# Residual with tokens on partitions, tokens stationary in the output and down projections, and another order in the prologue

## The chip, the cores and the metric

The kernel runs on one core of a Trainium2 chip. The core has a matrix engine (TensorE, PE in the profile), a vector engine (VectorE, DVE), an activation engine (ScalarE, ACT), a general engine (GpSimd, POOL) and a queue for transfers (SyncE, SP), which work side by side and wait for each other by semaphores. The metric is the time of one launch on the device in microseconds; several runs are made and their median is given.

## The reference

Two encoder layers over 256 tokens of 2048 features, float32. In each layer the normalised residual goes through one input projection (4608 columns), whose columns feed two groups of eight heads; the normalised outputs of the groups go through one output projection into the residual; a gated feed-forward part with a width-3 convolution over the tokens follows.

```python
for l in range(DEPTH):                                  # DEPTH = 2
    h = rms_norm(x, ln1_g[l])
    qa, ka, va, qb, kb, vb = jnp.split(h @ w_in[l], cuts, axis=-1)
    oa = neighborhood_attention(norm(qa), norm(ka), va, rpb[l])
    ob = windowed_gqa_sink(rope(norm(qb)), rope(norm(kb)), vb, sink[l])
    o = jnp.concatenate([rms_norm(oa, on_a[l]), rms_norm(ob, on_b[l])], axis=-1)
    x = x + o @ w_out[l]
    h2 = rms_norm(x, ln2_g[l])
    u = depthwise_conv(h2 @ w_up[l], conv_w[l], conv_b[l])
    gate, up = u[..., :D_FF], u[..., D_FF:]             # D_FF = 5632
    x = x + (jax.nn.silu(gate) * up) @ w_down[l]
```

(`norm` stands here for the RMS norm of each head with its gain.)

## The kernel before

**Products in two parts.** Every operand of the four projections is split into a high part and a low part, which both have the shorter mantissa of the format that PE takes in one pass (float32r): ACT copies the high part, DVE subtracts it to get the low part (`split`, lines 96 to 104). A product of two such operands is the sum of three products: high x high, high x low, low x high.

**Layout.** The residual `x` lies with features on partitions: 16 blocks of 128 features, each 256 tokens wide. `prep_x` (L123) makes the operands `xs[k]` of the next projection from block k, with the norm's gain folded in, and `square_x` (L118) adds the block's squares into `acc_x`; the norm's factor is applied after the projection. `stat_cols` (L130) and `stat_bcast` (L137) get that factor by products with a matrix of ones, as a column for each token or spread over the partitions.

**Two forms of product.** In the input projection (`q_win`, L363) the tokens are stationary: 128 tokens of `xs[k]` are loaded as weights, and 512 columns of the weight block move, three products for each block of features and token tile. The result has tokens on partitions. In the output, up and down projections (`q_wout` L413, `q_up` L452, `q_down` L495) the weights are stationary, 128 x 128 of them, and the tokens move. `two` (L356) issues there a pair: the high weights meet high and low tokens (512 columns), and the low weights meet the high tokens (256 columns). The sums come out in two halves of a bank, with features on partitions, and are added by `add_halves` (L444) or by two additions (`fin`, L512).

**The stream of weight blocks.** Weights come as blocks ("quanta") of at most 1 MiB in the order of `quanta`: in each layer nine jobs of four blocks for the input projection (`JOBS`, first the keys and values of group b), eight blocks of output projection for group b and eight for a, then four chunks of 11 feed-forward blocks (two weight blocks each), each followed by 16 smaller blocks of the down projection. One more up block is put before each chunk's down projection, so that PE has work while the last gate is computed; where there is none, in the last chunk, the halves of the first three down blocks are used in another order (`late`). `load` (L554) keeps three blocks in flight, `split_w` (L565) splits half a block four halves ahead of its use, and the loop at L620 walks through the halves ("steps"). Smaller work, such as the attention of one head, is put between the halves with `at` (L353). The order on each engine is planned when the kernel is built, from these priorities and a simulated timeline, so that a piece may stand a few instructions after the place where it was written.

**The gate.** `glu` (L474) takes an up block's pair of halves, adds them, multiplies by the norm's factor (on POOL, but for a layer's last block), convolves, gates and splits the result into `gs[f]`.

**Prologue.** `load_x` brings the residual in pieces between the first weight blocks, all on SP's queue. `prep_x` splits the 16 blocks on ACT and DVE, POOL squares them, and `rope_base` (L145) computes the rotary tables with some 40 DVE operations, placed at block 1. The first job, `kvb`, needs these tables when it is done.

**Tail.** In the last layer `fin` adds and stores two feature blocks at a time, and single ones at the very end.

Of the kernel before, what the change touches and what calls it, by code (L numbers as in the profile page):

```python
# [18 lines left out]
P = 128  # L19
L = 2  # L20
# [12 lines left out]
CH = 11  # L33
NCH = NF // CH
EPS = 1e-6
NEG = -1e30
JOBS = ("kvb", "qb0", "qb1", "va0", "ka0", "qa0", "qa1", "ka1", "va1")
# [9 lines left out]
def encoder_kernel(  # L47
# [18 lines left out]
    x = const.tile([P, KD, T], F32, name="x")  # L66

    def load_x(k, n):
        nc.sync.dma_start(out=x[:, k:k + n, :], in_=a["x"][:, k:k + n, :])  # L69
# [13 lines left out]
    def rsqrt(ps, inv_n, dst, tag):  # L83
        """dst = 1 / sqrt(ps * inv_n + EPS)"""
        n = list(dst.shape)
        v = work.tile(n, F32, name="v_" + tag, bufs=1)
        nc.vector.tensor_scalar(v, ps, inv_n, EPS, op0=ALU.mult, op1=ALU.add)
        nc.vector.tensor_scalar(dst.bitcast(I32), v.bitcast(I32), -0.5, 1597463007.0,
                                op0=ALU.mult, op1=ALU.add)
        t = work.tile(n, F32, name="t_" + tag, bufs=1)  # L90
        for _ in range(3):
            nc.vector.scalar_tensor_tensor(t, dst, -0.5, dst, op0=ALU.mult, op1=ALU.mult)
            nc.vector.tensor_mul(t, t, v)
            nc.vector.scalar_tensor_tensor(dst, t, 1.5, dst, op0=ALU.add, op1=ALU.mult)

    def split(hi, lo, src, scale=None):
        """hi + lo = src (* scale), each with float32r's mantissa"""
        if scale is None:
            nc.scalar.activation(hi, src, AF.Copy)  # L99
            nc.vector.tensor_sub(lo, src, hi.bitcast(F32))  # L100
        else:
            nc.scalar.activation(hi, src, AF.Copy, scale=scale)
# [3 lines left out]
    def add_square(acc, src, first, on_pool=False):  # L106
        sq = acc if first else work.tile([P, T], F32, name="sq", bufs=2)
        if on_pool:
            nc.gpsimd.tensor_mul(sq, src, src)
        else:  # L110
            nc.scalar.activation(sq, src, AF.Square)  # L111
# [6 lines left out]
    def square_x(k, on_pool=False):  # L118
        if k == 0:
            st["acc"] = act.tile([P, T], F32, name="acc_x")  # L120
        add_square(st["acc"], x[:, k, :], k == 0, on_pool)

    def prep_x(l, which, k, squares=True):  # L123
        """the operands of the next projection from one block of the residual"""
        xs[k] = act.tile([P, 2, T], F32R, name=f"xs{k}")
        split(xs[k][:, 0], xs[k][:, 1], x[:, k, :], ln_g[:, which, l, k:k + 1])
        if squares:
            square_x(k)

    def stat_cols(l):  # L130
        ps = psum.tile([P, TT], F32, name="pv", bufs=1)
        for tt in range(TT):
            mm(ps[:, tt:tt + 1], st["acc"][:, tt * P:(tt + 1) * P], ones[:, 0:1], True, True)
        st["r1"] = act.tile([P, TT], F32, name="r1")
        rsqrt(ps, 1.0 / D, st["r1"], "c2")

    def stat_bcast(acc, n, dst):  # L137
        ps = psum.tile([P, T], F32, name="pv", bufs=1)
        mm(ps, ones, acc, True, True)
        rsqrt(ps, 1.0 / n, dst, "b")  # L140

# [1 line left out]
    rope = {}  # L143

    def rope_base():  # L145
        """cos and sin of positions * inv, with the angle reduced exactly"""
# [3 lines left out]
        tmp = work.tile([P, 4, HD], F32, name="qtok", bufs=3)  # L150
# [6 lines left out]
        # 2 pi to 80 bits, in pieces of 7 bits  # L157
# [15 lines left out]

        nearest(k1, r, 4096.0)
        nc.vector.tensor_copy(r1, r)
        for c in pieces[:5]:
            less(r1, k1, c)
        nearest(k2, r1, 1.0)
        for c in pieces:
            less(r, k1, c)  # L180
            less(r, k2, c)
        nearest(k1, r, 1.0)
        for c in pieces[:5]:
# [13 lines left out]
    def rope_tables(l):  # L197
        """the rotation with the gains of the QK norm and the score scale folded in"""
# [18 lines left out]
    def evac_v(ps, cols, key):  # L217
        v = act.tile([P, TT, len(range(*cols.indices(512)))], F32, name="v_" + key[0], bufs=1)
        for tt in range(TT):
            nc.scalar.activation(v[:, tt, :], ps[tt][:, cols], AF.Copy, scale=st["r1"][:, tt:tt + 1])  # L220
        V[key] = v

    def evac_qk(ps, nh, kind):
        """QK norm and, for group b, the rotation; tokens on partitions"""
# [4 lines left out]
        for tt in range(TT):  # L229
            q = work.tile([P, 4, HD], F32, name="qtok", bufs=3)[:, :nh, :]  # L230
            nc.scalar.activation(q, ps[tt][:, :n].rearrange("p (h d) -> p h d", h=nh), AF.Copy,
# [117 lines left out]
    quanta = []  # L349
    late = []  # L350
# [10 lines left out]
    cur = {}  # L361

    def q_win(l, j, u):  # L363
        def body(q, half, hi, lo):
            if u == 0 and half == 0:
                cur["in"] = psum.tile([P, TT, 512], F32, name="mm", bufs=2)
            ps = [cur["in"][:, tt] for tt in range(TT)]
            hv, lv = (w.rearrange("p (k n) -> p k n", k=2) for w in (hi, lo))
            for tt in range(TT):
                for kk in range(2):  # L370
                    k = 4 * u + 2 * half + kk
                    x_h, x_l = (xs[k][:, i, tt * P:(tt + 1) * P] for i in range(2))
                    mm(ps[tt], x_l, hv[:, kk], k == 0, False)
                    mm(ps[tt], x_h, hv[:, kk], False, False)
                    mm(ps[tt], x_h, lv[:, kk], False, k == KD - 1)
# [4 lines left out]
            if u == 2 and j == 0:  # L380
                rope_tables(l)
            if u == 3 and j == 0:
                stat_cols(l)
            if u == 3:
                done_win(q, l, j, ps)
# [27 lines left out]
    def q_wout(l, grp, npair):  # L413
        def body(q, half, hi, lo):
            g = 0 if grp == "a" else 1
            if half == 0:
                cur["out"] = psum.tile([P, 2, 2, T], F32, name="mm", bufs=2)
            ps = cur["out"]
            hv, lv = (w.rearrange("p (k j n) -> p k j n", k=4, j=2) for w in (hi, lo))
            for j in range(2):  # L420
                for hh in range(4):
                    h = 4 * half + hh
                    two(ps[:, j], hv[:, hh, j], lv[:, hh, j], os[g * NH + h], h == 0, h == NH - 1)
            if half == 0:
                return
            if npair == 0:
                st["ro"] = act.tile([P, T], F32, name="ro", bufs=2)
                stat_bcast(acc_o[grp], NH * HD, st["ro"])
            if npair == KD // 2 - 1:
                with tc.high_priority(offset=4 * AHEAD_PRIO):  # L430
                    add_out(l, grp, 2 * npair, ps)
            else:
                add_out(l, grp, 2 * npair, ps)
        return body

    def add_out(l, grp, n, ps):
        t = add_halves(ps)
        nc.vector.tensor_mul(t, t, st["ro"][:, None, :].to_broadcast([P, 2, T]))
        nc.vector.tensor_add(x[:, n:n + 2, :], x[:, n:n + 2, :], t)
        if grp == "a":  # L440
            for j in range(2):
                prep_x(l, 1, n + j)

    def add_halves(ps):  # L444
        t = work.tile([P, 2, T], F32, name="prob", bufs=2)
        nc.scalar.activation(t, ps[:, :, 0], AF.Copy)  # L446
        nc.vector.tensor_add(t, t, ps[:, :, 1])  # L447
        return t
# [3 lines left out]
    def q_up(l, f, u):  # L452
        def body(q, half, hi, lo):
# [8 lines left out]
            if half == 0:  # L462
                return
            if u == 1 and f == 0:
                st["r2"] = act.tile([P, T], F32, name="r2")
                stat_bcast(st["acc"], D, st["r2"])
            if u == 1 and f == NF - 1:
                with tc.high_priority(offset=4 * AHEAD_PRIO):
                    glu(l, f, ps, nc.vector)
            elif u == 1:  # L470
                glu(l, f, ps, nc.gpsimd)
        return body

    def glu(l, f, ps, eng):  # L474
        t = add_halves(ps)
# [4 lines left out]
        eng.tensor_copy(ux[:, :, 1:r], ux[:, :, T:T + r - 1])  # L480
        eng.tensor_copy(ux[:, :, T + r:T + 2 * r - 1], ux[:, :, r + 1:2 * r])
# [13 lines left out]
    def q_down(l, c, n):  # L495
        def body(q, half, hi, lo):
            k0 = half * (CH // 2 + 1)
            hv, lv = (w.rearrange("p (k n) -> p k n", n=P) for w in (hi, lo))
            last = l == L - 1 and c == NCH - 1 and n >= KD - 2
            if (n % 2 == 0 or last) and half == 0:  # L500
                cur["dn", n // 2, last and n] = psum.tile([P, 2, 2, T], F32, name="mm", bufs=2)
            ps = cur["dn", n // 2, last and n]
            for kk in range(hv.shape[1]):
                k = k0 + kk
                two(ps[:, n % 2], hv[:, kk], lv[:, kk], gs[c * CH + k], k == 0, k == CH - 1)
            if half == 1 and last:
                fin(l, c, n, 1, ps[:, n % 2:n % 2 + 1])
            elif half == 1 and n % 2 == 1:
                fin(l, c, n - 1, 2, ps)
        return body  # L510

    def fin(l, c, n, m, ps):  # L512
        xv = x[:, n:n + m, :]
# [194 lines left out]
```

## Time and profile before

| what | value |
|---|---|
| median of 3 runs | 2141.22 us (2140.93 to 2141.46) |
| span of the profiled execution | 2139.1 us; the profile gives no time outside of the span for it |
| PE busy | 2119.9 us (99%) |
| DVE, ACT, POOL busy | 1566.4, 1179.8, 313.1 us |
| moved by DMA | 395.94 MB, mean 185 GB/s |

The span runs from the first to the last instruction; the runs' time is that of the launch, 2.1 us longer in the median. "Busy" is the time in which an engine executed at least one instruction. A group of instructions is given with its source line, its output and inputs by the program's names (`mm<-xs,whi`: the bank `mm` from the operands `xs` and `whi`), its shape, its count, its busy time and the mean duration of one. Products overlap on PE, so the mean duration of one is longer than the distance from one to the next; the distance is read from a stretch's length and its count. A product of plain float32 operands stands in the trace as two records.

### The profile page before, as it was taken

The numbers are of one execution on the slowest core, as the hardware profiler recorded it, in microseconds if no ns is written. First come the engines' busy times: TensorE is split into PE (matmuls) and PEld (weight loads), VectorE is DVE, ScalarE is ACT, GpSimd is POOL, SyncE is SP. The second block draws the span as 40 slices with busy tenths as digits, with TensorE's granted clock in tenths as the row PEclk, the third lists the DMA queues.
The fourth block names the chain that finished last, engine by engine and source line by source line (L and its number), as shares of the span: only waits on it lengthen the run. The fifth ranks groups of instructions, "written<-read, shape, count | busy, mean of one in ns | idle before, by whom it ended". The sixth has DMA issues, their size and how long they took to land.

```text
span 2139.1 us, 31086 instructions
## 1 busy us (share of the span) xinstructions
PE 2119.9 (99%) x11740; PEld 1848.2 (86%) x11740; DVE 1566.4 (73%) x2439; ACT 1179.8 (55%) x1744; POOL 313.1 (15%) x373
## 2 busy tenths in 40 slices
PE   7999999999999999999999999999999999999999
PEld 5888888888888888888888888888888888888888
DVE  8776789776677677667877667897766766776775
ACT  4665556654555455455656655565545545554553
POOL 5000013210121022012100100122102201110210
PEclk9999999999999999999999999999999999999999
DMA  7535555545654654654664454555465556546544
GB/s 260 191 131 179 175 179 179 197 166 197 208 185 166 220 181 168 212 191 157 199 215 176 141 187 164 177 182 194 168 212 191 179 176 217 192 161 219 188 157 167
DMA packets 64950, 395.94 MB, mean 185 GB/s; under 512 B 7840, under 2 KB 10144, under 8 KB 29088
## 3 DMA queue, kind: packets, MB, share of 16 engines
q1 hardware_dynamic: 64800, 393.96, 54.1%
q8 instruction: 92, 1.51, 0.3%
q14 instruction: 58, 0.48, 0.1%
HBM read 391.83 MB, written 2.10 MB: 184 GB/s over the span
## 4 chain that ended last, share of the span: by engine, by line
PE 98%; DVE 1%; DMA 1%; SPq 0%; ACT 0%; issue 0%
PE mm L81 95%; PE pv L81 1%; PE S L81 1%; PE tr L264 1%; DMA raw<-in_w_in 1%; PE tr L325 0%; PE tr L81 0%; DVE xs L103 0%; DVE wlo L100 0%; PE tr L320 0%; SPq L69 0%; SPq L561 0%; PE tr L317 0%; DVE qtok L172 0%; DVE qtok L153 0%
## 5 line engine op out<-in xcount | busy, mean ns | idle before, releaser
L100 DVE TENSOR_TENSOR wlo<-raw,whi 128x1024 fp32r<-128x1024 f32 (+3 forms) x817 | 944.8, 1157 | 496.6 <-ACT whi L99 490.0
L99 ACT ACTIVATE whi<-raw 128x1024 fp32r<-128x1024 f32 (+3 forms) x817 | 795.6, 975 | 803.3 <-PE mm L81 656.2
L81 PE MATMUL mm<-xs,whi 128*128 128x512 f32 x2816 | 976.5, 391 | 0.0
L81 PE MATMUL mm<-xs,wlo 128*128 128x256 f32 x2816 | 788.8, 280 | 0.0
L81 PE MATMUL mm<-mid,whi 128*128 128x512 f32 x1920 | 670.1, 392 | 0.0
L81 PEld LDWEIGHTS mm<-xs,whi 128*128 128x128 f32 x2816 | 526.5, 187 | 115.4
L81 PE MATMUL mm<-mid,wlo 128*128 128x256 f32 x1920 | 541.7, 282 | 0.0
L81 PEld LDWEIGHTS mm<-xs,wlo 128*128 128x128 f32 x2816 | 532.2, 189 | 0.1
L81 PEld LDWEIGHTS mm<-mid,whi 128*128 128x128 f32 x1920 | 360.7, 188 | 75.6 <-DVE prob L447 0.4
L81 PE MATMUL mm<-whi,xs 128*128 128x512 f32 x1152 | 369.7, 399 | 6.9 <-ACT whi L99 6.9
L81 PEld LDWEIGHTS mm<-mid,wlo 128*128 128x128 f32 x1920 | 362.9, 189 | 0.2
L478 POOL TENSOR_TENSOR halo<-prob,r 128x512 f32<-128x512 f32 x86 | 112.0, 1303 | 1094.4 <-DVE prob L447 1069.7
L81 PEld LDWEIGHTS mm<-whi,xs 128*128 128x128 f32 x1152 | 216.5, 190 | 50.5 <-ACT whi L99 7.2
L81 PE MATMUL mm<-wlo,xs 128*128 128x512 f32 x576 | 230.1, 399 | 8.1 <-DVE wlo L100 8.1
L488 DVE SCALAR_TENSOR_TENSOR pT<-halo,conv,pT 128x256 f32<-128x256 f32 x352 | 149.6, 486 | 6.4
L81 PEld LDWEIGHTS mm<-wlo,xs 128*128 128x128 f32 x576 | 109.2, 190 | 32.6 <-DVE wlo L100 10.4
L486 ACT ACTIVATE pT<-halo,conv 128x256 f32<-128x256 f32 x176 | 96.3, 595 | 40.7 <-POOL halo L478 40.4
L480 POOL COPY halo<-halo 128x6 f32<-128x6 f32 x86 | 85.0, 989 | 5.5
L447 DVE TENSOR_TENSOR prob<-prob,mm 128x512 f32<-128x512 f32 x120 | 81.6, 680 | 0.0
L113 POOL TENSOR_TENSOR acc_x<-acc_x,sq 128x256 f32<-128x256 f32 x60 | 55.8, 930 | 144.7 <-ACT sq L111 142.4
L446 ACT ACTIVATE prob<-mm 128x512 f32<-128x512 f32 x120 | 69.7, 581 | 0.0
L113 POOL TENSOR_TENSOR acc_b<-acc_b,sq 128x256 f32<-128x256 f32 x14 | 16.4, 1171 | 284.1 <-ACT sq L111 284.1
(132 smaller groups left out, 987.4 us busy)
## 6 DMA issues: line engine op xcount, KB each, us to landing
raw<-in_w_up SPq DMA_DIRECT2D x176, 1024.0 KB, 4.8
raw<-in_w_down SPq DMA_DIRECT2D x128, 704.0 KB, 4.1
raw<-in_w_in SPq DMA_DIRECT2D x71, 1024.0 KB, 4.8
raw<-in_w_out SPq DMA_DIRECT2D x32, 1024.0 KB, 4.8
bias<-in_bias SPq DMA_DIRECT2D x16, 160.0 KB, 2.3
out<-x SPq DMA_DIRECT2D x7, 256.0 KB, 4.1
x<-in_x SPq DMA_DIRECT2D x3, 512.0 KB, 9.7
raw<-in_w_in SPq DMA_DIRECT2D x4, 256.0 KB, 5.9
```

Source lines behind the costliest of these rows:

```text
L81: nc.tensor.matmul(ps, lhsT, rhs, start=start, stop=stop, skip_group_check=True)
L99: nc.scalar.activation(hi, src, AF.Copy)
L100: nc.vector.tensor_sub(lo, src, hi.bitcast(F32))
L113: nc.gpsimd.tensor_add(acc, acc, sq)
L264: nc.tensor.transpose(ps[:, j, tt * P:(tt + 1) * P], qn[tt][:, p + j, :], ident)
L446: nc.scalar.activation(t, ps[:, :, 0], AF.Copy)
L447: nc.vector.tensor_add(t, t, ps[:, :, 1])
L478: eng.tensor_mul(ux[:, :, r:r + T], t, st["r2"][:, None, :].to_broadcast([P, 2, T]))
L480: eng.tensor_copy(ux[:, :, 1:r], ux[:, :, T:T + r - 1])
L486: nc.scalar.activation(y[:, j, :], ux[:, j, r:r + T], AF.Identity, scale=w1, bias=b)
L488: nc.vector.scalar_tensor_tensor(y[:, j, :], ux[:, j, o:o + T], w, y[:, j, :], op0=ALU.mult, op1=ALU.add)
```

## The change

The residual lies with tokens on partitions (two tiles of 128 tokens, 2048 wide). The output and down projections take the input projection's form: `three` issues, for two blocks of the contraction at a time, the products high x high, low x high and high x low, each with 128 tokens stationary and 512 columns of weights moving, into two banks. The result is added to the residual straight from the banks, by `add_x`. `whole_x` follows where a quarter of the residual (512 features, `nb`) is complete: `square_x` sums its squares on ACT by row, and `turn_x` transposes it on PE, 128 x 128 at a time, into a bank from which `prep_x` makes the operands of the next projection. `stat_x` computes the norm's factor; for the up projection it spreads it over the partitions with one product.

The down projection has chunks of 12, 12, 12 and 8 feed-forward blocks and weight blocks of 1 MiB throughout; `late` is gone, and the last chunk takes its first two quarters in turns. The gate's multiplication is on DVE for all blocks.

In the prologue the transposed input comes as an input of its own (`xT`), half of it on ACT's queue; ten small products of ones stand ahead on PE; the first job is `va0`, which needs no tables; the residual itself is loaded later, held behind the issue of certain weight loads (`issue_after`), and is squared on ACT; `rope_base` yields pieces that are spread over blocks 4 and 5; the first job's eviction is put off to block 7.

```diff
-JOBS = ("kvb", "qb0", "qb1", "va0", "ka0", "qa0", "qa1", "ka1", "va1")
+JOBS = ("va0", "kvb", "qb0", "qb1", "ka0", "qa0", "qa1", "ka1", "va1")
...
+    x = const.tile([P, TT, D], F32, name="x")
...
+    def square_x(nb):
...
+        for tt in range(TT):
+            sq = work.tile([P, 512], F32, name="sqx", bufs=1)
+            nc.scalar.activation(sq, x[:, tt, nb * 512:(nb + 1) * 512], AF.Square,
+                                 accum_out=st["ss"][:, tt, nb:nb + 1])
+
+    def turn_x(l, which, nb):
+        for k in range(4 * nb, 4 * nb + 4, 2):
+            ps = psum.tile([P, 2, T], F32, name="S", bufs=2)
+            for j in range(2):
+                for tt in range(TT):
+                    nc.tensor.transpose(ps[:, j, tt * P:(tt + 1) * P], x[:, tt, (k + j) * P:(k + j + 1) * P], ident)
+            for j in range(2):
+                prep_x(l, which, k + j, ps[:, j, :])
+
+    def stat_x(which):
+        v = work.tile([P, TT], F32, name="ssum", bufs=2)
+        nc.vector.reduce_sum(v, st["ss"], axis=AX.X)
+        st["r1"] = act.tile([P, TT], F32, name="r1")
+        rsqrt(v, 1.0 / D, st["r1"], "c2")
+        if which == 1:
...
+            mm(ps, ones, d[:, 0:TT].rearrange("p t d -> p (t d)"), True, True)
...
+    def three(ps, terms, hv, lv, first, last):
+        n = len(terms)
+        for x_part, w in ((0, hv), (1, hv), (0, lv)):
+            for tt in range(TT):
+                for i, x2 in enumerate(terms):
+                    mm(ps[:, tt], x2[:, x_part, tt * P:(tt + 1) * P], w[:, i],
+                       first and w is hv and x_part == 0 and i == 0, last and w is lv and i == n - 1)
...
             if u == 3:
-                done_win(q, l, j, ps)
+                if l == 0 and j == 0:
+                    at(q + 4, done_win, q, l, j, ps, half=0)
+                else:
+                    done_win(q, l, j, ps)
...
+    def whole_x(q, l, which, nb, ps, r=None):
+        with tc.high_priority(offset=4 * AHEAD_PRIO if nb == NB - 1 else 0):
+            add_x(nb, ps, r)
+        at(q + 1, square_x, nb, half=0)
+        at(q + 1, turn_x, l, which, nb, half=0)
+        if nb == NB - 1:
+            at(q + 1, stat_x, which)
...
-        eng.tensor_mul(ux[:, :, r:r + T], t, st["r2"][:, None, :].to_broadcast([P, 2, T]))
+        nc.vector.tensor_mul(ux[:, :, r:r + T], t, st["r2"][:, None, :].to_broadcast([P, 2, T]))
...
+            else:
+                for tt in range(TT):
+                    xv = x[:, tt, nb * 512:(nb + 1) * 512]
+                    nc.vector.tensor_add(xv, xv, ps[:, tt])
+                    nc.sync.dma_start(out=out[:, tt, nb * 512:(nb + 1) * 512], in_=xv)
...
+            if end == NF:
+                order = sorted(order, key=lambda o: (o[0] // 2, o[1], o[0]) if o[0] < 2 else (1, 0, 0))
...
+    for i in range(KD // 2):
+        xT.append(act.tile([P, 2, T], F32, name="mid", bufs=16))
+        if i < 4:
+            nc.scalar.dma_start(out=xT[i], in_=a["xT"][:, 2 * i:2 * i + 2, :])
...
+    load(0, 4)
+    for i in range(4, KD // 2):
+        nc.sync.dma_start(out=xT[i], in_=a["xT"][:, 2 * i:2 * i + 2, :])
+        if i % 2:
+            load(i // 2 - 1)
...
+    def load_x(nb):
+        n = slice(nb * 512, (nb + 1) * 512)
+        with tc.issue_after(loads[LOAD_AHEAD + nb].ins):
+            nc.sync.dma_start(out=x[:, :, n], in_=a["x"][:, :, n])
...
+    for i in range(10):
+        mm(ps[:, 0:P], ones, ones, True, True)
...
+    for nb in range(NB):
+        at(1 + nb, load_x, nb, half=0)
+        at(3 + nb, square_first, nb, half=0)
+    at(7, stat_x, 0, half=0)
+    at(5, load_rest)
+    turn = rope_base()
+    for i in range(12):
+        at(4 + i // 6, next, turn, None, half=(i // 3) % 2)
```

More of the change, by code (lines that the diff above doesn't have):

```diff
@@ L116, in encoder_kernel, with prep_x @@
     st = {}
[L118 to L123, printed above, removed]
-        xs[k] = act.tile([P, 2, T], F32R, name=f"xs{k}")
[L126 to L130, printed above, removed]
+    def prep_x(l, which, k, src):
+        xs[k] = act.tile([P, 2, T], F32R, name=f"xs{k}")
+        split(xs[k][:, 0], xs[k][:, 1], src, ln_g[:, which, l, k:k + 1])
@@ L359, in two, with banks @@
         mm(ps[:, 1], w_l, mv[:, 0], False, last)
+    def three(ps, terms, hv, lv, first, last):
[5 more added lines that the diff above has]
+                       first and w is hv and x_part == 0 and i == 0, last and w is lv and i == n - 1)
     cur = {}
+    def banks(key, first):
+        if first:
+            cur[key] = psum.tile([P, TT, 512], F32, name="mm", bufs=2)
+        return cur[key]
     def q_win(l, j, u):
         def body(q, half, hi, lo):
-            if u == 0 and half == 0:
-                cur["in"] = psum.tile([P, TT, 512], F32, name="mm", bufs=2)
-            ps = [cur["in"][:, tt] for tt in range(TT)]
+            ps = banks("in", u == 0 and half == 0)
             hv, lv = (w.rearrange("p (k n) -> p k n", k=2) for w in (hi, lo))
[L369 to L375, printed above, removed]
+            k = 4 * u + 2 * half
+            three(ps, (xs[k], xs[k + 1]), hv, lv, k == 0, k == KD - 2)
             if half == 0:
@@ L415, in body @@
             g = 0 if grp == "a" else 1
[L416 to L425, printed above, removed]
@@ L444, in add_halves @@
[L444 to L448, printed above, removed]
+            ps = banks("out", u == 0 and half == 0)
+            hv, lv = (w.rearrange("p (k n) -> p k n", k=2) for w in (hi, lo))
+            h = 4 * u + 2 * half
+            three(ps, (os[g * NH + h], os[g * NH + h + 1]), hv, lv, h == 0, h == NH - 2)
+            if nb == 0 and u == 0 and half == 1:
+                stat_o(grp)
@@ new lines, in body @@
+            if u == 1 and half == 1:
+                if grp == "b":
+                    add_x(nb, ps, st["ro"])
+                else:
+                    whole_x(q, l, 1, nb, ps, st["ro"])
+        return body
+    def whole_x(q, l, which, nb, ps, r=None):
[5 more added lines that the diff above has]
+            at(q + 1, stat_x, which)
@@ L493, in glu, with q_down @@
         split(gs[f][:, 0], gs[f][:, 1], t[:, 1, :])
-    def q_down(l, c, n):
+    def q_down(l, c, nb, g):
+        f0, nf = sum(CHUNKS[:c]), CHUNKS[c]
         def body(q, half, hi, lo):
[L497 to L509, printed above, removed]
-        return body
-    def fin(l, c, n, m, ps):
-        xv = x[:, n:n + m, :]
-        nc.vector.tensor_add(xv, xv, ps[:, :, 0])
-        nc.vector.tensor_add(xv, xv, ps[:, :, 1])
-        if c == NCH - 1:
-            if l + 1 < L:
-                for j in range(m):
-                    prep_x(l + 1, 0, n + j)
-            else:
-                nc.sync.dma_start(out=out[:, n:n + m, :], in_=xv)
+            ps = banks(("dn", nb), g == 0 and half == 0)
+            hv, lv = (w.rearrange("p (k n) -> p k n", k=2) for w in (hi, lo))
+            i = FG * g + 2 * half
+            three(ps, (gs[f0 + i], gs[f0 + i + 1]), hv, lv, i == 0, i == nf - 2)
+            if g < nf // FG - 1 or half == 0:
+                return
+            if c < len(CHUNKS) - 1:
+                add_x(nb, ps)
+            elif l + 1 < L:
+                whole_x(q, l + 1, 0, nb, ps)
+            else:
+                for tt in range(TT):
+                    xv = x[:, tt, nb * 512:(nb + 1) * 512]
+                    nc.vector.tensor_add(xv, xv, ps[:, tt])
+                    nc.sync.dma_start(out=out[:, tt, nb * 512:(nb + 1) * 512], in_=xv)
+        return body
     for l in range(L):
@@ L545, in encoder_kernel @@
-    steps = []
-    for q, (_, n, _) in enumerate(quanta):
-        m = n // 2 if n == 2048 else (CH // 2 + 1) * P
-        steps += [(q, 0, slice(0, m)), (q, 1, slice(m, n))]
-    for q in late:
-        steps[2 * q:2 * q + 6] = [steps[2 * q + i] for i in (0, 2, 4, 1, 3, 5)]
-    raw, hl, left = {}, {}, {}
-    def load(q, parts=1, between=None):
+            for nb in range(NB):
+                for u in range(2):
+                    quanta.append((a["w_out"][l, 0 if grp == "a" else 1, nb, u], q_wout(l, grp, nb, u)))
@@ new lines, in encoder_kernel @@
+        f = 0
+        for c, nf in enumerate(CHUNKS):
+            end = min(sum(CHUNKS[:c + 1]) + 1, NF)
+            while f < end:
+                for u in range(2):
+                    quanta.append((a["w_up"][l, f, u], q_up(l, f, u)))
+                f += 1
+            ng = nf // FG
+            order = [(nb, g) for nb in range(NB) for g in range(ng)]
+            if end == NF:
+                order = sorted(order, key=lambda o: (o[0] // 2, o[1], o[0]) if o[0] < 2 else (1, 0, 0))
+            for nb, g in order:
+                quanta.append((a["w_down"][l, sum(CHUNKS[:c]) // FG + g, nb], q_down(l, c, nb, g)))
@@ L555, in load @@
+    steps = [(q, h) for q in range(len(quanta)) for h in range(2)]
+    raw, hl, left, loads, highs = {}, {}, {}, {}, {}
+    def load(q, parts=1):
         if q < len(quanta):
-            src, n, _ = quanta[q]
-            raw[q] = wp.tile([P, 2048], F32, name="raw", bufs=3)[:, :n]
+            raw[q] = wp.tile([P, 2048], F32, name="raw", bufs=3)
             left[q] = 2
-            m = n // parts
+            m = 2048 // parts
             for j in range(parts):
-                nc.sync.dma_start(out=raw[q][:, j * m:(j + 1) * m], in_=src[:, j * m:(j + 1) * m])
-                if between and j == 0:
-                    between()
+                loads[q] = nc.sync.dma_start(out=raw[q][:, j * m:(j + 1) * m], in_=quanta[q][0][:, j * m:(j + 1) * m])
@@ L565, in split_w @@
     def split_w(s, parts=1):
         if s < len(steps):
-            q, _, sl = steps[s]
-            n = sl.stop - sl.start
-            hl[s] = tuple(wp.tile([P, 1024], F32R, name=t, bufs=SPLIT_AHEAD + 1)[:, :n] for t in ("whi", "wlo"))
-            m = n // parts
+            q, half = steps[s]
+            hl[s] = tuple(wp.tile([P, 1024], F32R, name=t, bufs=SPLIT_AHEAD + 1) for t in ("whi", "wlo"))
+            m = 1024 // parts
             for j in range(parts):
-                with tc.high_priority(offset=AHEAD_PRIO):
-                    split(*(t[:, j * m:(j + 1) * m] for t in (*hl[s], raw[q][:, sl])))
+                with tc.high_priority(offset=AHEAD_PRIO if s >= KD // 2 else 0):
+                    highs[s] = split(*(t[:, j * m:(j + 1) * m] for t in hl[s]),
+                                     raw[q][:, half * 1024 + j * m:half * 1024 + (j + 1) * m])
@@ L603, in encoder_kernel @@
         nc.gpsimd.memset(prob_a[i], 0.0)
-    for k in range(KD):
-        if k < 12:
-            prep_x(0, 0, k, squares=False)
-        else:
-            at(0, prep_x, 0, 0, k, False)
-        if k % 3 == 0 and k // 3 < SPLIT_AHEAD:
-            split_w(k // 3, 2 if k == 0 else 1)
-        square_x(k, on_pool=True)
+    ps = psum.tile([P, T], F32, name="pv", bufs=1)
+    for i in range(10):
+        mm(ps[:, 0:P], ones, ones, True, True)
+    for i in range(SPLIT_AHEAD):
+        first_x(i)
+        split_w(i, 2 if i == 0 else 1)
     for n, shape, dt, src in (
```

160 lines of the change are left out of this document (71 added, 89 removed).

## The prediction

> **What bounds the kernel now.** I read the first page's totals and its chain, then what TensorE (PE) waited for, then stretches in which only one kind of product runs.
>
> ```profile
> span 2139.1 us, 31086 instructions
> ...
> PE 2119.9 (99%) x11740; PEld 1848.2 (86%) x11740; DVE 1566.4 (73%) x2439; ACT 1179.8 (55%) x1744; POOL 313.1 (15%) x373
> ...
> PE 98%; DVE 1%; DMA 1%; SPq 0%; ACT 0%; issue 0%
> ```
> ```profile
> PE mm L81 <- DVE wlo L100: 8.1, 4, 6.1
> PE mm L81 <- ACT whi L99: 6.9, 1, 6.9
> ```
>
> PE is the chain for 98% of the span. The waits table (total, times, longest) gives it 15.0 us of waiting, and the timeline below puts the two long pieces before 37 us. After that PE has no gaps: only the number and the pace of its own instructions count, and cheaper work on DVE, ACT or POOL is worth nothing there by itself. So I price the change in PE time, and the prologue apart.
>
> The pace, from three stretches that hold nothing else (the columns after the window are its length and each engine's busy time with its count; the code has 352, 96 and 704 products in the first three, and the windows count two or three more whose modelled ends reach in):
>
> ```profile
> 1016.79:1077.81 61.02, 61.02 (x355) 54.09 (x354) 51.95 (x70) 38.26 (x65) 10.81 (x13) 1.00 0.62 209
> 1077.81:1099.58 21.77, 21.77 (x98) 18.02 (x97) 13.40 (x13) 9.93 (x13) 1.81 (x2) 1.00 0.64 233
> 539.74:661.77 122.03, 122.03 (x706) 107.59 (x705) 85.40 (x117) 68.69 (x94) 24.55 (x30) 1.00 0.54 183
> 306.00:360.00 54.00, 54.00 (x311) 47.53 (x310) 52.27 (x71) 35.34 (x60) 14.41 (x15) 1.00 0.54 180
> ```
>
> The first is one down-projection chunk: 176 pairs of a 512- and a 256-column product in 61.02 us, **346.7 ns a pair**. The second is the first input job of layer 1: 96 products of 512 columns with tokens stationary in 21.77 us, **226.8 ns each**. The third, up-projection, has the pair again (352 pairs, 346.7 ns).
>
> **The change, part by part.**
>
> *Output and down projections.* These are the groups that change form:
>
> ```profile
> L81 PE MATMUL mm<-mid,whi 128*128 128x512 f32 x1920 | 670.1, 392 | 0.0
> L81 PE MATMUL mm<-mid,wlo 128*128 128x256 f32 x1920 | 541.7, 282 | 0.0
> ```
>
> The 1920 pairs (512 output, 1408 down) become the input projection's form: four 128-wide output blocks, so far 4 pairs = 1386.8 ns, become 3 terms x 2 token tiles = 6 products of 512 columns = 1360.8 ns. That is 26.0 ns for each of 1920 / 4 = 480: **-12.5 us**. The streamed columns are the same (3072), so only the fixed part of each instruction shrinks, six instead of eight. The other end is nothing at all: if cost followed columns, a new product would take 346.7 x 2/3 = 231.1 ns. I take 226.8, the row of the same operand kinds and sizes. The order of products is new too, in the input projection as well (two into one bank, then two into the other). No row shows it; I take 0, and bound it at 1 ns either way for 1728 + 2880 products, 4.6 us.
>
> *Turning the residual.* 16 blocks x 2 token tiles, three times (twice to the up, once to layer 1's input projection): 96 transposes. The chain has the like:
>
> ```profile
> 129.35 0.44 PE tr L264 x4
> 129.78 1.73 PE S L81 x8
> ```
>
> Four take 0.44 us between products: 96 x 0.11 = **+10.6 us**, all on PE. Nothing hides it, since PE has no idle time left there; it cannot be a gain. More than that needs a wait (last rival).
>
> *Statistics.* A 128x256 fp32 product is two of the S records above, 1.73 / 8 x 2 = 0.43 us; four one-column records took 0.34 us (below). Removed: six of the former and two groups of the latter, 3.3 us; added: two and four, 2.2. **-1.1 us**.
>
> *Prologue.* The chain and the timeline up to 43 us, and windows of 4 us:
>
> ```profile
> 1.18 0.42 SPq L69
> ...
> 36.08 6.65 PE mm L81 x22
> 42.73 0.34 PE pv L81 x4
> ```
> ```profile
> 4.13 1.28 ACT L102 ACT_TABLE_LOAD   x1 [4.13 <-DMA x<-in_x]
> ...
> 6.91 1.22 PE L81 MATMUL mm<-whi,xs 128*128 128x512 f32 x2 [6.91 <-ACT whi L99]
> ...
> 36.08 0.79 PE L81 MATMUL mm<-wlo,xs 128*128 128x512 f32 x1 [6.09 <-DVE wlo L100]
> ```
> ```profile
> 0.00:4.00 4.00, 0.00 (x0) 0.00 (x0) 0.17 (x2) 0.00 (x0) 3.05 (x11) 1.00 0.40 123
> 4.00:8.00 4.00, 1.09 (x2) 0.50 (x2) 2.03 (x3) 3.51 (x6) 2.72 (x5) 1.00 0.84 263
> 12.00:16.00 4.00, 4.00 (x13) 3.13 (x12) 4.00 (x6) 3.23 (x6) 3.92 (x5) 1.00 1.00 419
> 32.00:36.00 4.00, 0.00 (x0) 0.00 (x0) 3.90 (x9) 0.04 (x1) 1.61 (x3) 0.52 0.00 0
> ```
>
> The first job's 96 products end at 42.6 us and need 21.8 at full pace: 20.8 us are lost to the 6.9 us start, the 6.1 us wait for a low part that stood behind the rotary arithmetic on DVE, a granted clock that the idle stretch cut to 0.52, and smaller waits. The change takes the rotary pieces out of the first job (it needs none: va0), spreads them over blocks 4 and 5, takes the squares off POOL, and keeps PE busy with ten small products from about 1 us. What is late next is DMA. Tokens (2 KB rows) and the first block (2 KB rows) go at the 263 GB/s of the 4 to 8 us window, whole blocks at 419. Ahead of block 1 stand 2.5 MiB = 2.62 MB: 0.49 MB by 4 us (123 GB/s), the rest by 12.1, block 1 by 14.6, its high part (1.06 us, below) by 15.7. Blocks 2 and 3 then land at 19.1 and 21.6, before PE wants them. The last 72 products x 226.8 ns end at 32.0: **-10.6 us**. The first 24 products lie before that; even at half pace (24 x 0.45 = 10.9, from 5.7) they are only 0.9 late.
>
> Ends of that term: with no DMA wait PE starts at 5.7 (4.13 for tokens, two operands of 0.50 and a half-width high part of about 0.6 on ACT, rows below) and ends at 27.5, -15.1; if a DVE wait of 6.1 us comes back somewhere in blocks 0 to 7, -4.5. Queues: ACT gets four DMA issues (0.42 each, as on SP) and the table load, 3.0 us, done by the time that tokens land. On SP the four residual loads of 0.5 MiB are held until blocks 3 to 6 are issued, and stand before the next weight issues; blocks run three ahead of PE, 16 us, so that 1.2 us of data each delay nobody. va0's eviction, held to block 7, frees its banks for block 8, one half-block (2.72 us) before that, against two evictions on ACT of about 0.63 each (the like is below).
>
> *DVE, ACT, POOL.* The groups that move:
>
> ```profile
> L100 DVE TENSOR_TENSOR wlo<-raw,whi 128x1024 fp32r<-128x1024 f32 x559 | 707.4, 1266 | 348.6 <-ACT whi L99 342.7 <-ACT pT L321 2.5 <-ACT kT L266 2.0
> L447 DVE TENSOR_TENSOR prob<-prob,mm 128x512 f32<-128x512 f32 x120 | 81.6, 680 | 0.0
> L514 DVE TENSOR_TENSOR x<-x,mm 128x512 f32<-128x512 f32 x63 | 43.3, 687 | 11.4 <-PE mm L81 11.4
> L439 DVE TENSOR_TENSOR x<-x,prob 128x512 f32<-128x512 f32 x32 | 23.5, 736 | 0.4
> L92 DVE SCALAR_TENSOR_TENSOR t_qk<-r_qk 128x8 f32<-128x8 f32 x36 | 6.5, 179 | 0.8
> L102 ACT ACTIVATE xs<-x,ln_g 128x256 fp32r<-128x256 f32 x64 | 30.9, 500 | 18.6 <-DVE x L439 15.3 <-DVE x L515 3.2
> L99 ACT ACTIVATE whi<-raw 128x1024 fp32r<-128x1024 f32 x559 | 591.5, 1060 | 549.1 <-PE mm L81 422.4 <-issue 106.4 <-DMA raw<-in_w_in 7.9
> L234 ACT ACTIVATE tq<-qtok 128x512 f32<-128x512 f32 x24 | 14.7, 634 | 0.1
> ```
>
> Output: 32 x (0.68 + 2 x 0.74) = 69 us of DVE become 32 adds of about 0.74 = 24. Down: 126 adds of 0.69 = 87 become 32 of twice the width, about 42. The gate's multiplication of 512 columns, 84 times, comes over from POOL: 84 x 0.68 = +57. Net about -33, and POOL loses its adds. The last chunk of a layer has no up block behind it to cover the gate's last block; its cover was 18 pairs (6.2 us) and is now 60 products (13.6 us): 0. All this lies beside PE (a half-block of 12 products is 2.72 us on PE, 1.27 on DVE, 1.06 on ACT) and counts 0; were DVE the bound, the 57 us alone would show.
>
> *Tail.* So far two 128x256 adds (0.42 each) and a 128 KB store end the span.
>
> ```profile
> 2134.92 0.42 DVE L514 TENSOR_TENSOR x<-x,mm 128x256 f32<-128x256 f32 x1 [2.93 <-PE mm L81]
> 2135.38 0.42 DVE L515 TENSOR_TENSOR x<-x,mm 128x256 f32<-128x256 f32 x1
> 2135.83 0.33 SPq L521 DMA_DIRECT2D out<-x  x1
> ```
> ```profile
> out<-x SPq DMA_DIRECT2D x7, 256.0 KB, 4.1
> ```
>
> The last store is issued at 2135.83 and lasts to 2139.1, 3.3 us. After: two 128x512 adds (0.69), the first partly under the last products, then 256 KB at 4.1: +0.5 to +1.3, I take **+0.9**.
>
> **Sum:** -12.5 + 10.6 - 1.1 - 10.6 + 0.9 = -12.7 us, span 2126.4. The median of the runs, 2141.22, is 2.1 above the profiled span; I keep that: **2128.5 us**. In the steady part gain and cost cancel almost (-3.0); the prologue carries the forecast.
>
> **Rivals.**
>
> *The new form is no faster per column* (231.1 ns): sum -0.2, 2141.0. For it: the columns are the same, and one form's row alone speaks for the smaller figure. Against: two stretches of this same trace at clock 1.00 give 346.7 against 226.8. The Trainium skill (TensorE: Matmul & The Clock Gate, Wait — 56ns, not 53.3ns?) puts a warm product at N / 2.4 ns plus about 2.5: 325.0 a pair and 215.8 a product, an estimated gain of 2.5 us in place of 12.5, so 2138.5, within this rival's range. The trace disagrees with both figures (346.7 and 226.8).
>
> *The prologue gives little*: a 6.1 us DVE wait returns, -4.5 for -10.6, 2134.6. For it: DVE was busy for 3.90 of 4 us while PE stood. Against: the rotary pieces now fall where PE has four half-blocks in hand.
>
> *PE waits at the turns*, and the kernel is slower. The turn stands 12 products (2.72 us) behind the block whose sum it reads. Two adds on DVE take 1.47. With two low parts ahead of them (2.5) PE waits 1.3 us, twelve times: +15.6, 2144.1. With three, since the splits have priority and run up to four half-blocks ahead, it is 2.6 each, +30.7, 2159.2. Everything queued behind on PE would wait too. The old time is reached at 12.7 / 12 = 1.06 us a turn, 0.2% above it at 1.4. For it: DVE is 52.27 of 54.00 us busy in layer 0's output stage (fourth window). Against: the attention's transposes depend on DVE in the same way, and the waits table shows PE no wait for them: they were placed a few products later.
>
> **How the numbers follow.** Forecast 0.60, own range 2121 to 2136. Little from the prologue 0.17 (2131 to 2137). No faster form 0.12 (2137 to 2144). Waits at the turns 0.08 (0.06 of it beyond 2145.5). The remaining 0.03 is other small mishaps from 2139 up, a third of them over 2145.5. A measurement of this kernel tells about 0.2% (4.3 us) from no change. Faster 0.77, same 0.16, slower 0.07. The range runs from 2119 (the prologue's good end, -4.5, and the new order's, -4.6, from 2128.5) to 2140, which leaves out the turns and part of the no-faster case.
>
> **What would show it.** A down chunk of 12 blocks: 288 products in 65.3 us (66.6 if the form is no faster). The transposes of x: 96 records, about 10.6 us, with no PE wait before them. The first 96 products done by about 32 us, with waits only for loads. POOL without multiplications. What would make it wrong: PE waits after 40 us, or a first job that ends after 38.

## The result and the profile after

The changed kernel takes 2145.91 us (median of 15 runs, 2145.31 to 2146.87), the kernel before, in the same series, 2141.74 (2140.93 to 2142.64). The ratio is 1.002, with an interval of 1.0012 to 1.0028. The forecast was 2128.5 and faster; the kernel is 4 us slower.

The first page of the changed kernel, its chain's shares, and the table of what PE waited for (total, times, longest):

```profile
span 2143.6 us, 28784 instructions
...
PE 2135.8 (100%) x10896; PEld 1812.2 (85%) x10896; DVE 1462.1 (68%) x2291; ACT 1141.5 (53%) x1651; POOL 66.0 (3%) x215
...
PE 99%; DMA 0%; SPq 0%; DVE 0%; ACT 0%; DVEq 0%; issue 0%
```
```profile
PE mm L80 <- ACT whi L98: 2.4, 2, 1.4
PE pv L80 <- DVE halfpi L76: 1.1, 1, 1.1
```

PE is still the chain, and its waits have shrunk from 15.0 to 3.5 us, none of them at a turn. It executes 844 instructions fewer, and yet its busy time rose by 16 us: the time came from the pace of its own work. So the next view is that of the stretches. Three windows of the changed kernel, two up stretches (384 pairs each) and a down chunk of 12 blocks (288 products); the columns here are the length, PE's busy time and count, the granted clock, the DMA share and GB/s:

```profile
547.89:683.56 135.67, 135.67 (x770) 1.00 0.54 186
748.85:884.52 135.67, 135.67 (x770) 1.00 0.54 186
482.58:547.89 65.31, 65.31 (x291) 1.00 0.56 195
```

The down chunk is as forecast: 65.31 / 288 = 226.8 ns. But the **up projection, whose code the change leaves alone**, takes 135.67 / 384 = 353.3 ns a pair; before, it took 346.7. For 2816 pairs that is +18.6 us. Its clock is granted in full, and it waits for nothing. The starts in the timeline, before and after at about the same time, show that the gap is in every few instructions (start, modelled duration):

```profile
599.95 0.28 PE L81 MATMUL mm<-xs,wlo 128*128 128x256 f32 x1
600.07 0.39 PE L81 MATMUL mm<-xs,whi 128*128 128x512 f32 x1
600.30 0.28 PE L81 MATMUL mm<-xs,wlo 128*128 128x256 f32 x1
600.41 0.39 PE L81 MATMUL mm<-xs,whi 128*128 128x512 f32 x1
600.64 0.28 PE L81 MATMUL mm<-xs,wlo 128*128 128x256 f32 x1
```
```profile
600.05 0.28 PE L80 MATMUL mm<-xs,wlo 128*128 128x256 f32 x1
600.17 0.40 PE L80 MATMUL mm<-xs,whi 128*128 128x512 f32 x1
600.40 0.28 PE L80 MATMUL mm<-xs,wlo 128*128 128x256 f32 x1
600.52 0.40 PE L80 MATMUL mm<-xs,whi 128*128 128x512 f32 x1
600.76 0.28 PE L80 MATMUL mm<-xs,wlo 128*128 128x256 f32 x1
```

Before, from the first low product to the third it is 0.69 us; after, 0.71. In the trace's nanoseconds the distances before are 230 and 117, pair after pair. After, they repeat every three pairs: 232, 118, 241, 120, 236, 113, which makes 1060 ns instead of 1040. This runs through whole stretches without a change: it is a steady rhythm, not a disturbance now and then.

### The profile page after: what moved, and what is told of

It is laid out like the page before. It is cut to its first block, busy times and chain, and to the rows that moved or that the text cites. A ratio compares the mean times of both kernels' runs of the same rounds, so it can differ in the third digit from the quotient of the medians.

```text
span 2143.6 us, 28784 instructions
## 1 busy us (share of the span) xinstructions
PE 2135.8 (100%) x10896; PEld 1812.2 (85%) x10896; DVE 1462.1 (68%) x2291; ACT 1141.5 (53%) x1651; POOL 66.0 (3%) x215
## 4 chain that ended last, share of the span: by engine, by line
PE 99%; DMA 0%; SPq 0%; DVE 0%; ACT 0%; DVEq 0%; issue 0%
PE mm L80 95%; PE pv L80 1%; PE S L80 1%; PE tr L286 1%; PE S L134 0%; PE tr L347 0%; PE tr L80 0%; DMA raw<-in_w_in 0%; PE tr L342 0%; PE tr L339 0%; DVE x L533 0%; ACT whi L98 0%; DVEq L747 0%; SPq L571 0%; SPq L64 0%
## 5 line engine op out<-in xcount | busy, mean ns | idle before, releaser
L99 DVE TENSOR_TENSOR wlo<-raw,whi 128x1024 fp32r<-128x1024 f32 (+1 forms) x737 | 901.8, 1224 | 558.4 <-ACT whi L98 522.3
L98 ACT ACTIVATE whi<-raw 128x1024 fp32r<-128x1024 f32 (+1 forms) x737 | 779.8, 1059 | 885.8 <-PE mm L80 682.4
L80 PE MATMUL mm<-whi,mid 128*128 128x512 f32 x1920 | 481.0, 391 | 0.0
L80 PEld LDWEIGHTS mm<-whi,mid 128*128 128x128 f32 x1920 | 358.0, 188 | 72.8
L80 PE MATMUL mm<-whi,xs 128*128 128x512 f32 x1152 | 297.7, 396 | 2.4 <-ACT whi L98 2.4
L80 PE MATMUL mm<-wlo,mid 128*128 128x512 f32 x960 | 259.3, 390 | 0.0
L80 PEld LDWEIGHTS mm<-wlo,mid 128*128 128x128 f32 x960 | 180.1, 188 | 37.2
L80 PE MATMUL mm<-wlo,xs 128*128 128x512 f32 x576 | 162.0, 396 | 0.0
L499 DVE TENSOR_TENSOR halo<-prob,r 128x512 f32<-128x512 f32 x88 | 60.9, 692 | 2.7
L501 POOL COPY halo<-halo 128x6 f32<-128x6 f32 x88 | 17.7, 201 | 1454.7 <-DVE halo L499 1454.7
```

The costliest lines, as they stand in the source:

```text
L80: nc.tensor.matmul(ps, lhsT, rhs, start=start, stop=stop, skip_group_check=True)
L98: high = nc.scalar.activation(hi, src, AF.Copy)
L499: nc.vector.tensor_mul(ux[:, :, r:r + T], t, st["r2"][:, None, :].to_broadcast([P, 2, T]))
L501: nc.gpsimd.tensor_copy(ux[:, :, 1:r], ux[:, :, T:T + r - 1])
```

## The experiments

Three theories for the slow rhythm were possible from these traces. The `junk` tile of the new prologue is 4 bytes wide and takes 32, so it moves all weight blocks and operands behind it by 32 bytes (A: addresses). The ten early products take the first bank of the sum memory, so the projections' sums moved from banks 0-3 to 1-4 (B: banks). Or traffic of the other engines is to blame (C). All experiments compare with the kernel before on the same chip.

### E1: everything 32 bytes further

```diff
-            nc.scalar.activation(const.tile([P, 1], F32, name="junk"), halfpi, AF.Copy)
+            nc.scalar.activation(const.tile([P, 16], F32, name="junk")[:, 0:1], halfpi, AF.Copy)
```

> The changed kernel with one unused scratch tile made 64 bytes wide instead of 4, so that everything allocated behind it, weight blocks and operands included, lies 32 bytes further in each partition (weights and up operands at 32 modulo 64, as in the kernel before). Theory A (the pace of a weights-stationary pair depends on these addresses): the up pair falls from 353.5 ns to 346.7, 2816 pairs make -19 us, median about 2127, the form with tokens stationary stays at 226.7 to 227. Theory B (the banks of the sums, which the early products moved from 0-3 to 1-4) and theory C (traffic of other engines in the up stage): no change, up pair 353.5, about 2146.

Measured: 2140.64 us, ratio 0.9995 (0.9986 to 1.0004). Windows of the first up stretch of layer 0 and of the next one:

```profile
346.26:480.45 134.19, 134.19 (x775) 1.00 0.55 189
545.76:681.43 135.67, 135.67 (x770) 1.00 0.55 186
```

The first has 773 records, 347.2 ns a pair; the next has the slow rhythm, as have all later ones of the layer; layer 1 repeats it. Two of the eight stretches became faster, with the same addresses as the other six. No theory had forecast this. Theory A in its plain form is refuted: one program, one set of addresses, two paces.

### E2: the sums back in banks 0-3

```diff
-    ps = psum.tile([P, T], F32, name="pv", bufs=1)
+    ps = psum.tile([P, TT, 512], F32, name="mm", bufs=2)
     for i in range(10):
-        mm(ps[:, 0:P], ones, ones, True, True)
+        mm(ps[:, 0, 0:P], ones, ones, True, True)
```

> The changed kernel with its ten early products written into the projections' own sum tile, so that these sums lie in banks 0-3 again, as before the change; addresses in the operand memory unchanged. Theory B: up pair 346.7 ns, median about 2127. Theory A and C: no change, 353.5 ns, about 2146.

Measured: 2145.67 us, ratio 1.0018 (1.0009 to 1.0027).

```profile
548.22:683.89 135.67, 135.67 (x769) 1.00 0.55 186
```

The pace is that of the changed kernel. Theory B is refuted.

### E3: the kernel before, moved by 32 bytes

```diff
     nc.vector.memset(halfpi, math.pi / 2)
+    nc.vector.memset(const.tile([P, 1], F32, name="pad"), 0.0)
```

> The kernel before with one 4-byte tile more ahead of the weights, which puts weights and up operands at 0 modulo 64 bytes and the down operands at 32, all else unchanged. Theory A: up pair from 346.7 to 353.5 ns, +19 us, about 2161; if the weights' address alone decides, the 1920 output and down pairs slow down too, together +32 us, about 2174. Theory B and C: no change, about 2141.7.

Measured: 2141.43 us, ratio 0.9999 (0.9990 to 1.0009).

```profile
541.10:663.13 122.03, 122.03 (x706) 1.00 0.53 183
```

352 pairs in 122.03 us, 346.7 ns: no change. In this kernel, the place of the operands as such is not it.

### E4: the operands moved against the weights

```diff
+    nc.vector.memset(act.tile([P, 1], F32, name="pad"), 0.0)
     xT = []
```

> The changed kernel with a 4-byte tile ahead of the operands alone: weights stay at 0 modulo 64, the operands of the up projection and the gated values go to 32. Theory A: if the weights' own address decides, up pair stays 353.5 ns, about 2146; if weights and moving operand must not both lie at 0, it falls to 346.7, about 2127. Theory B and C: no change.

Measured: 2153.43 us, ratio 1.0057 (1.0043 to 1.0070). An up stretch and a down chunk:

```profile
553.38:686.52 133.14, 133.14 (x770) 1.00 0.56 189
486.18:553.38 67.20, 67.20 (x290) 1.00 0.57 190
```

The pair is fast again, 133.14 / 384 = 346.7 ns, in every stretch (347.1 in the first of each layer), and the token-stationary form became slow, 67.20 / 288 = 233.3 ns. E1 moved the operands by the same 32 bytes, and the weights with them, and six of its eight stretches stayed slow. So what counts here is the **distance** between weights and operands, which E1 and E3 left alone. Theory C falls with it, since the other engines and transfers do the same work beside it. By the addresses that the kernels allocate, the distance from weights to up operands is a multiple of 1 KB in the kernel before, and that to the down operands is 32 bytes more than a multiple of 512; in the changed kernel, all are multiples of 1 KB.

What was left to explain is why the up projection, at a multiple of 1 KB before and after, is fast before. Theory P: at this distance the pair has several rhythms, and the one that it falls into is set where the stretch is entered. Before, PE comes to it from other pairs; after, from token-stationary products.

### F2: the up projection's weights moved

The tiles of the split weights become 1040 wide in place of 1024, and those of up blocks begin 8 floats in.

```diff
-            hl[s] = tuple(wp.tile([P, 1024], F32R, name=t, bufs=SPLIT_AHEAD + 1) for t in ("whi", "wlo"))
+            o = 8 if q in ups else 0
+            hl[s] = tuple(wp.tile([P, 1040], F32R, name=t, bufs=SPLIT_AHEAD + 1)[:, o:o + 1024] for t in ("whi", "wlo"))
```

> The changed kernel, the split weights of the up projection alone 32 bytes further in their tile, so that they lie at 32 modulo 64 against the moving operand's 0; input, output and down weights stay at 0 as their stationary operands. Theory R (the distance of stationary and moving operand modulo 64 bytes sets the pattern; at 32 the pair has one pattern of 346.7 to 346.9 ns however it is entered, at 0 it has a fast and a slow one, and the token-stationary form wants 0): up pair 346.8 in all stretches, other products 226.7 to 227, -19 us, about 2127. Rival (E4's gain came from the place of the operands as such): up pair stays 353.5, 2146.

Measured: 2153.38 us, ratio 1.0055 (1.0041 to 1.0068).

```profile
552.11:686.08 133.97, 133.97 (x770) 1.00 0.55 188
485.34:552.11 66.77, 66.77 (x291) 1.00 0.57 191
```

Pair 348.9 ns, product 231.8: a miss on both, for the theory and for its rival. The edit did two things. The five buffers now lie 4160 bytes apart instead of 4096, so that their distances to the operands differ by multiples of 64 bytes; for the token-stationary form this is the only change, and it does not keep its 226.8 ns at such distances, so "modulo 64" was too coarse. For the pair the 32 bytes come on top, and this run does not separate the two.

### F3: a break ahead of the up stretches

```diff
                 cur["up"] = psum.tile([P, 2, 2, T], F32, name="mm", bufs=2)
+                if f in (2, 13, 25, 37):
+                    ps = psum.tile([P, 2, T], F32, name="tr", bufs=1)
+                    for i in range(4):
+                        nc.tensor.transpose(ps[:, i // 2, i % 2 * P:(i % 2 + 1) * P], ident, ident)
```

> The changed kernel with four small transposes of the identity matrix (into the bank that the attention's transposes use, result unused) put ahead of the third up block of a layer and of the first one behind each of its down chunks: 32 records, about 3.6 us. Theory P (the pair has several repeating patterns at the same addresses, and which one runs is set where it is entered): some or all of the eight up stretches change their pattern there and run at 346.7 to 348 ns instead of 353.5; all eight would make 2146 + 3.6 - 19, about 2131. Rival (addresses alone): 353.5 everywhere, about 2149.

Measured: 2149.55 us, ratio 1.0036 (1.0023 to 1.0050).

```profile
548.94:684.69 135.75, 135.75 (x772) 1.00 0.54 185
```

No stretch changed. By itself this spoke for the rival; but a break need not lead into another rhythm, so it could not decide.

### F4: the kernel before, entered from the other form

```diff
                 cur["up"] = psum.tile([P, 2, 2, T], F32, name="mm", bufs=2)
+                if f in (2, 12, 23, 34):
+                    ps = psum.tile([P, 2 * T], F32, name="tr", bufs=1)
+                    for i in range(6):
+                        mm(ps, xs[i][:, 0, 0:P], hi[:, 0:512], True, True)
```

> The kernel before with six products of the token-stationary form (result unused, into the bank of the attention's transposes) put ahead of the third up block of a layer and of the first one behind each of its down chunks: 48 products, 10.9 us. Theory P: entered from these products the pair falls into the slow pattern, 353.5 ns, as in the changed kernel; all eight stretches would make 2141.7 + 10.9 + 19, about 2171; at least one changes. Rival (layout or traffic of the changed kernel): 346.7 everywhere, about 2152.6.

Measured: 2166.33 us, ratio 1.0114 (1.0100 to 1.0128). First the windows of two up stretches, behind the six products at the third block and behind those at the first down chunk's end; then the timeline where the second begins:

```profile
369.93:480.86 110.93, 110.93 (x641) 1.00 0.52 177
543.26:667.62 124.36, 124.36 (x706) 1.00 0.52 176
```
```profile
541.76 0.28 PE L81 MATMUL mm<-mid,wlo 128*128 128x256 f32 x1
541.88 1.54 PE L81 MATMUL tr<-whi,xs 128*128 128x512 f32 x6
543.26 0.39 PE L81 MATMUL mm<-xs,whi 128*128 128x512 f32 x1
543.48 0.28 PE L81 MATMUL mm<-xs,wlo 128*128 128x256 f32 x1
543.60 0.40 PE L81 MATMUL mm<-xs,whi 128*128 128x512 f32 x1
543.83 0.28 PE L81 MATMUL mm<-xs,wlo 128*128 128x256 f32 x1
543.95 0.40 PE L81 MATMUL mm<-xs,whi 128*128 128x512 f32 x1
544.19 0.28 PE L81 MATMUL mm<-xs,wlo 128*128 128x256 f32 x1
544.31 0.40 PE L81 MATMUL mm<-xs,whi 128*128 128x512 f32 x1
```

The six products at 541.88 end within 1.5 us, and the 704 that follow take 124.36 us: 353.3 ns a pair, the slow rhythm, in the kernel that the change has not touched, at its own addresses. The first stretch, entered from the same six products, stays at 110.93 / 320 = 346.7. Of the eight stretches six are slow, 2048 pairs: 2048 x 6.6 ns = 13.5, and 10.9 for the products themselves, on 2141.89: 2166.3, as measured. So **the entry decides, and the rhythm then stays for a hundred microseconds**. The form ahead is not the whole rule, though, since the first stretch of each layer stays fast behind the same six products. In the changed kernel too the rhythm turns at breaks. Its chain in the first up block of layer 0 (start, length, what):

```profile
329.08 9.94 PE mm L80 x49
339.02 0.22 PE S L134 x2
339.24 0.35 PE mm L80 x2
339.59 0.65 PE S L134 x6
340.24 5.58 PE mm L80 x32
345.82 0.43 PE pv L80 x2
346.25 3.76 PE mm L80 x21
```

Behind the transposes 32 records take 5.58 us, 348.8 ns a pair; behind the statistic's product (345.82) it is the slow rhythm again, to the chunk's end.

### G1: a distance at which the pair has one rhythm

The 16 operands come into one tile, 2 KB apart as before; those for the up projection are written and read 32 bytes further than those for the input projection, and no weights move.

```diff
-        xs[k] = act.tile([P, 2, T], F32R, name=f"xs{k}")
+        if "all" not in xs:
+            xs["all"] = act.tile([P, KD * 2 * T + 16], F32R, name="xs")
+        o = k * 2 * T + 8 * which
+        xs[k] = xs["all"][:, o:o + 2 * T].rearrange("p (i t) -> p i t", i=2)
```

> The changed kernel with the 16 operands xs in one tile, 2 KB apart as before, and those for the up projection written and read 32 bytes further than those for the input projection. All weight blocks stay where they are. Theory R as mended by the last run (what counts is the distance between stationary and moving operand; multiples of 1 KB suit the token-stationary form, a rest of 32 bytes leaves the pair one pattern of 346.8 ns however it is entered): up pair 346.8 ns in all eight stretches, other products 226.7 to 227, -19 us, median about 2127. Rival (a fast pair and a fast token-stationary form exclude each other, as in the two runs with shifts so far): one of them is slow, 353.5 or above 231 ns, 2146 or more.

Measured: **2128.11 us**, ratio 0.9935 (0.9922 to 0.9947). Its span, and an up stretch and a down chunk:

```profile
span 2126.3 us, 28784 instructions
```
```profile
546.35:679.49 133.14, 133.14 (x770) 1.00 0.56 190
481.06:546.35 65.29, 65.29 (x290) 1.00 0.57 194
```

Pair 346.7 ns, product 226.7, both at once; the other up stretches run alike. It executes the same instructions as the changed kernel, and takes 17.8 us less than the 2145.91 of the first series. It beats both kernels. The one tile without the 32 bytes was not run; that E4, with 16 tiles, has the same 346.7 ns at the same 32 bytes speaks for the place and not for the tile.

### G2: without the early products

```diff
-    ps = psum.tile([P, T], F32, name="pv", bufs=1)
-    for i in range(10):
-        mm(ps[:, 0:P], ones, ones, True, True)
```

> The kernel of the run before (g1) without the ten products of ones ahead of the first job. If they wake the clock in time, the first job's 96 products now end later than 31.3 us, by up to 2.5 us (12 products at half pace); if the first job waits for transfers anyway, it ends within 0.5 us of it. The pace of the rest stays: within 2.5 us of the run before.

Measured: 2127.86 us, ratio 0.9935 (0.9921 to 0.9948), with G1's 2128.11 within the scatter. The second job begins at 32.05 us, and at 32.30 in G1 (31.34 in the changed kernel), so without the ten products the first job ends no later: they buy nothing that these runs can tell. A window of the changed kernel (PE, PEld, DVE, ACT, POOL, clock, DMA share, GB/s), and PE's timeline in the changed kernel and in this run, show why:

```profile
8.00:12.00 4.00, 3.91 (x10) 3.10 (x11) 3.13 (x7) 3.48 (x9) 0.00 (x0) 0.58 1.03 393
```
```profile
4.81 0.39 PE L80 MATMUL pv<-ones 128*128 128x128 f32 x2
6.55 0.50 PE L80 MATMUL mm<-whi,xs 128*128 128x512 f32 x1 [1.36 <-ACT whi L98]
8.09 3.35 PE L80 MATMUL mm<-whi,xs 128*128 128x512 f32 x7 [1.04 <-ACT whi L98]
11.25 1.14 PE L80 MATMUL mm<-wlo,xs 128*128 128x512 f32 x4
```
```profile
8.13 3.35 PE L80 MATMUL mm<-whi,xs 128*128 128x512 f32 x7 [0.81 <-ACT whi L98]
11.29 1.84 PE L80 MATMUL mm<-wlo,xs 128*128 128x512 f32 x4
```

In the changed kernel the ten products end at 5.2 us, PE has one product to do until 8.09, and the granted clock is 0.58 in the next window: seven products take 3.35 us. Without the ten, seven take the same 3.35 us; the profile of G2 gives a clock of 1.00 there, so that its pace has to be read and not its clock. The next four take 1.14 us in the changed kernel, 1.84 here and 1.91 in G1, which has the ten products too: when the full pace comes back does not hang on them. The Trainium skill (TensorE: Matmul & The Clock Gate, What's actually happening) has a window of about 3.4 us of activity behind this gate; the half pace of the changed kernel, from 8.09 to about 11.25 us, agrees, and in G1 and G2 it lasts longer, to about 12.9.

## Why the prediction was wrong

**The step that failed** is the use of the third window: the up projection "has the pair again (352 pairs, 346.7 ns)", and the sum then has no term for it, with no reason given why its pace should stay. It went from 346.7 to 353.3 ns a pair and cost +18.6 us, more than the whole forecast gain of 12.7. What the runs showed in its place is that the pace of the same pairs at the same addresses depends on what PE executes just ahead of them (F4), at the distances between operands that the changed kernel has, and that 32 bytes of distance cure it (G1). That the change made the stretches slow by putting token-stationary products ahead of them is the reading that fits both; no run put pairs ahead of them in the changed kernel, so this last link is argued. No rival had this; the three of them stayed away, and so did both signs of being wrong that the prediction named.

The other terms came out within 1 us, with their rows above:

- Output and down products: 226.8 ns forecast, 226.8 measured. The rival by which cost follows columns (231.1) does not hold. Neither does the 215.8 that comes, as an estimate, out of the rule of the Trainium skill (TensorE: Matmul & The Clock Gate, Wait — 56ns, not 53.3ns?).
- Transposes: the chain has two in 0.22 us, six in 0.65, eight to a turn, twelve turns: 10.4 us against 10.6, and the waits table has no wait there, so the rival of waits at the turns did not happen.
- Statistics: the one product that spreads the factor takes the 0.43 us that was forecast (345.82 in F4's chain of the changed kernel).
- Prologue: the chain of the changed kernel from the second product on,

```profile
1.65 5.74 DMA raw<-in_w_in
...
8.09 24.09 PE mm L80 x98
```

  is PE alone: 98 products until 32.18 us, of which the last three belong to the second job. So the first job is done at about 31.4 us where 32.0 was forecast, with no wait for a load behind 8.09. The number came out, but by another way: the forecast had PE waiting for block 1 until 15.7 us, whereas PE came later itself, at half clock, and block 1 was there in time. That the two end so close is luck.
- Tail: +0.9 was forecast. The last products start at 2138.22, a row of four, and the span ends 4.3 us behind their end, where it was 4.2 before; so this term is about +0.1. A store of 256 KB takes 2.1 us on the page of the changed kernel, and not the 4.1 that was taken.
- DVE fell from 1566.4 to 1462.1 us, more than the 33 that I worked out, and it mattered as little as POOL's loss.

The sum without the failed step was 2126.4 us of span. G1, where that step is mended, has 2126.3. That it is so near is in part luck: the tail came out 0.8 us below its term, and G1's first job ends about 0.3 us later than forecast.

## What to carry to other kernels

When a change leaves a stage's code alone, check its pace all the same, by count and length of a stretch: on PE, the same instructions on the same data ran 2% slower, for more than 100 us at a time, because of the six instructions ahead of them. Where PE is the bound, compare the distance between stationary and moving operands as tiles are added or reordered; one small scratch tile or a wider buffer moves everything behind it. And sum PE time by stage before a change is dropped as worthless: this one was worth 0.65% with its 32 bytes, and cost 0.2% without.

## What the runs showed of the hardware

- Streams of products with their weight loads run in steady rhythms, and a pair of 512 and 256 columns has more than one at the same addresses: 346.7 ns, and 353.3 ns in a pattern of three pairs (the kernel before and F4). It keeps the one into which it fell at its entry, until something else is executed.
- The distance between the two operands has a part in which rhythms there are. At multiples of 1 KB: pair 346.7 to 353.3, token-stationary product 226.7 to 226.8. With the operands 32 bytes further: pair 346.7 in all long stretches of E4 and G1, product 233.3 (E4). With distances that differ by multiples of 64 bytes, and 32 on top for the pair (F2): 348.9 and 231.8.
- Moving both operands by 32 bytes changed nothing in the kernel before (E3), and in the changed one only the first stretch of each layer (E1).

What it is inside of PE or its memory that makes these rhythms was not tried, and neither was the rule for which entry leads to which; F3 shows that a break of four transposes does not help.
